# Dividing softmax weights ahead of their transposes in a hybrid attention layer

## The chip, the cores and the metric

The kernel runs on one core of a Trainium2 chip. The metric is the time of one execution on the device in microseconds, the median of three runs of the kernel. A profile is a further execution, recorded instruction by instruction. TensorE (PE) does matmuls and transposes, VectorE (DVE), ScalarE (ACT) and GpSimd (POOL) the elementwise work, and SyncE (SP) issues transfers. Each engine works through a queue of its own in a fixed order and waits on semaphores.

## The reference

One step of an encoder layer for 512 prompt rows and 64 sample rows (with 128 cached rows), 1024 wide: a projection, two kinds of attention with 8 heads of 64 each, an output projection, two layer norms, a feed-forward part of 4096 and a gated embedding.

```
def fox_attend(q, k, v, cum_q, cum_k, q_pos, k_pos):
    s = jnp.einsum('bqhd,blhd->bhql', q, k, ...) * HEAD_DIM ** -0.5
    decay = ...                       # sums of log forget gates, query less key
    p = jax.nn.softmax(jnp.where(mask, s + decay, NEG), axis=-1)
    return jnp.einsum('bhql,blhd->bqhd', p.astype(v.dtype), v)

def dsa_attend(q, k, v, iq, ik, iw, q_pos, k_pos, topk):
    # an indexer scores the keys: sum over index heads of iw * relu(iq . ik)
    _, sel = lax.top_k(score, topk)   # attention over the chosen keys alone
    ...
    x = layer_norm(ALPHA * x + jnp.einsum('blm,md->bld', mix, w_o), ln1_g, ln1_b)
    hid = jnp.square(jax.nn.relu(jnp.einsum('bld,df->blf', x, w_up)))
    x = layer_norm(ALPHA * x + jnp.einsum('blf,fd->bld', hid, w_down), ln2_g, ln2_b)
```

## The kernel before, in words

Prompt and sample are 576 columns, in two halves of 288. A float32 factor is split into a high part (rounded) and a low part (the rest), and each product is three matmuls (L274): high by high, high by low, low by high. Weights go through one queue of units: a load by SP (L155), a cast on ScalarE for the high part (L176), a subtraction on VectorE or, for some units, GpSimd for the low part (L180). The tiles are wraw and whl. Calls of WT.step(n) emit up to n such pieces between matmuls.

The heads are taken in eight pairs (p). Pairs 0 to 3 are forgetting attention, pairs 4 to 7 indexed attention. While pair p + 1 is projected (k, q, v, each 48 matmuls into one PSUM tile m), pair p is attended to by `ticks`: 9 jobs for each pair, prompt block i (128 queries, so 128 to 512 keys) of head hh, and one for the sample. A job passes through stages, one tick after another, in the order that PLAN writes out: qk (the scores, PSUM tile S), addmax (scores plus bias, and their maximum, on VectorE, L858), exp (ScalarE, L866, with the sum of the row), norm, ptrans (transposes of the weights sP into PSUM tile T), pevac (PT from T; ScalarE in pairs 0 to 3, VectorE in 4 to 7). After a pair's last job pv multiplies by the values into PSUM tiles V (prompt) and X (sample), and oevac writes the output's high and low parts, BH and BL. S, T and X share three PSUM banks.

Where the division lies: the sample's job divides its weights in norm (reciprocal L871, multiplication L872) ahead of its transposes. For the prompt the weights stay as they are. At a pair's last job, VectorE takes the reciprocals of all sums, ScalarE spreads them to 64 columns each (rows, L877), TensorE transposes them (four transposes, X<-ident,rows), ScalarE copies them out (R, L888), and oevac multiplies V by R (mix, L951); then ScalarE rounds mix to BH (L953) and GpSimd subtracts for BL (L954).

The evacuations of a projection (proj_evac) go into a list of delayed calls, of which three are made after each step of 6 matmuls. For q of pairs 1 to 3 these are: qs, the high part (ScalarE, L720), the low part (VectorE, L721), two pairs of transfers on SP's queue (L722, L723), the sample's queries QS out of the same m (ScalarE, L726), two casts on GpSimd (L727, L728).

Beside the first pairs runs the indexer (`choice`): its logits (L631 on TensorE, L634 a relu on ScalarE out of S or X, L637 and L639 a sum on VectorE), for the sample last (tiles cosT, sinT, dbiasS), and then top-k on VectorE (max, match_replace).

Behind pair 7: wo1 (six eighths of the output projection), wo2 for the halves A and B (the last two eighths; its evacuation, L1248, adds to Y and feeds the layer norm's sums), ple, the first feed-forward group, and so on. wo2 calls WT.step(4) after each of its 8 steps in half A and WT.step(0) in half B. A scheduler moves instructions within each engine's queue by its own estimate of times, so that the order below is not only that of the code.

Of the kernel before, what the change touches and what calls it, by code (L numbers as in the profile page):

```python
# [11 lines left out]
OP = mybir.AluOpType  # L12
# [24 lines left out]
def tile_hybrid_step(ctx: ExitStack, tc: tile.TileContext, I, O):  # L37
# [6 lines left out]
    def f(ap):  # L44
        return ap.bitcast(F32)
# [637 lines left out]
    def proj_evac(p, kind, m):  # L683
        g, pp = divmod(p, 4)
        v = m[:, :, :HW]
        P = pair[p]
        dly = [0]

        def q(fn, d=None):
            if d is not None:  # L690
                dly[0] = d
            later(dly[0], fn)

        def v2(ap):
# [12 lines left out]
        if g == 0:
            if kind == "q":
                P["q32s"] = QS[p % 2]
                P["Q2"] = Q2[p % 2]  # L710
                if p == 0:
                    q(lambda: ACT.mul(v2(QE[lo]), v[lo], sc))
                    q(lambda: ACT.mul(v2(QO[hi]), v[hi], sc))
                    q(lambda: DVE.scalar_tensor_tensor(v2(QE[hi]), v[lo], sc, f(v2(QE[lo])), op0=OP.mult, op1=OP.subtract))
                    q(lambda: DVE.scalar_tensor_tensor(v2(QO[lo]), v[hi], sc, f(v2(QO[hi])), op0=OP.mult, op1=OP.subtract))
                    src = (QE, QO)
                else:

                    qh, ql = [sb.tile([128, NT], F32R, name="qs", tag=t) for t in ("t2", "t1")]
                    q(lambda: ACT.mul(v2(qh), v, sc))  # L720
                    q(lambda: DVE.scalar_tensor_tensor(v2(ql), v, sc, f(v2(qh)), op0=OP.mult, op1=OP.subtract))  # L721
                    q(lambda: (SP.dma_start(f(QE[lo]), f(qh[lo])), SP.dma_start(f(QO[hi]), f(qh[hi]))))  # L722
                    q(lambda: (SP.dma_start(f(QE[hi]), f(ql[lo])), SP.dma_start(f(QO[lo]), f(ql[hi]))))  # L723
                    src = (qh, qh)
                for r in (lo, hi):
                    q(lambda r=r: ACT.mul(P["q32s"][r, r], m[r, 1, HW - NS:HW], sc))  # L726
                q(lambda: POOL.tensor_copy(P["Q2"][lo, 0], f(src[0][lo, :NP])))  # L727
                q(lambda: POOL.tensor_copy(P["Q2"][hi, 1], f(src[1][hi, :NP])))  # L728
                return
            k32 = sb.tile([128, NT], F32, name="k32", bufs=1)  # L730
            q(lambda: ACT.copy(v2(k32), v))
        else:
            state["k"] -= 4.0 if kind == "q" else 2.4
            x32 = sb.tile([128, NT], F32, name="x32", tag="k32" if kind == "k" else "t1")
            xr = sb.tile([128, NT], F32, name="xr", tag="t2")
            for r in range(4):
                s = r ^ 1
                q(lambda r=r, s=s: ACT.mul(v2(xr[r * 32:r * 32 + 32]), v[s * 32:s * 32 + 32], sc))
            q(lambda: DVE.scalar_tensor_tensor(v2(x32), v, sc, v2(cosT), op0=OP.mult, op1=OP.mult))
            q(lambda: DVE.tensor_tensor(xr, xr, sinT, OP.mult), 3)  # L740
            q(lambda: DVE.tensor_tensor(x32, x32, xr, OP.add), 3)
            if kind == "q":
                P["q32s"] = QS[p % 2]
                q(lambda: ACT.copy(QE[lo], x32[lo]), 5)
                q(lambda: ACT.copy(QO[hi], x32[hi]))
                q(lambda: DVE.tensor_tensor(QE[hi], x32[lo], f(QE[lo]), OP.subtract), 5)
                q(lambda: DVE.tensor_tensor(QO[lo], x32[hi], f(QO[hi]), OP.subtract))
                for r in (lo, hi):
                    q(lambda r=r: ACT.copy(P["q32s"][r, r], x32[r, NP:]))
                return  # L750
            k32 = x32
        P["k32"] = k32
        P["KL"] = KL = KLP[p % 2]
        P["k32s"] = sb.tile([128, NS], F32, name="k32s", bufs=2)
        q(lambda: ACT.copy(QE[lo], k32[lo]), 6 if g else 3)
        q(lambda: ACT.copy(QO[hi], k32[hi]))
        q(lambda: (SP.dma_start(f(QE[hi]), f(QE[lo])), SP.dma_start(f(QO[lo]), f(QO[hi]))))
        q(lambda: SP.dma_start(O["kT"][g, pp], k32))
        eng = POOL if p > 1 else DVE
        q(lambda: eng.tensor_tensor(KL[lo, 0], k32[lo, :NP], f(QE[lo, :NP]), OP.subtract))  # L760
        q(lambda: eng.tensor_tensor(KL[hi, 1], k32[hi, :NP], f(QO[hi, :NP]), OP.subtract))
        q(lambda: ACT.copy(P["k32s"], k32[:, NP:]))
# [97 lines left out]

    def exp(j):
        P = pair[j["p"]]
        if "sums" not in P:
            P["sums"] = sb.tile([128, 2, 4], F32, name="sums", bufs=2)
        s = j["st"][:, 2:3] if j["s"] else P["sums"][:, j["hh"], j["i"]:j["i"] + 1]
        ACT.activation(j["P"], j["P"], AF.Exp, bias=j["st"][:, 0:1], scale=-1.0, accum_out=s)  # L866

    def norm(j):

        if j["s"]:  # L870
            DVE.reciprocal(j["st"][:, 3:4], j["st"][:, 2:3])  # L871
            ACT.mul(j["P"], j["P"], j["st"][:, 3:4])  # L872
        elif j["last"]:
            sums = pair[j["p"]]["sums"]
            DVE.reciprocal(sums, sums)
# [2 lines left out]

    def scales(j):

        if not j["last"]:
            return
        rows = pair[j["p"]]["rows"]
        ps = psum_1("X", 1)
# [59 lines left out]
    def oevac(j):  # L944
# [485 lines left out]
    L1A = LayerNorm(A, 0, (4, 5, 2, 12))  # L1430
    L1B = LayerNorm(B, 0, (3, 8, 7, 12))
    L1 = both(L1A, L1B)
    drive(wo2(A, L1A, 4), 8, None, 0)
    early = fb.tile([128, 4], F32, name="ln_r", bufs=2)
    ACT.activation(early[:, 0:1], epst, AF.Sqrt, bias=epst[:, 0:1])
    drive(seq(wo2(B, L1B, 0), ple()), 24, L1, 24, False)
    drive(up(0, (L1A, L1B)), 16, L1, 16, False)
    XS = sums_of_x()
    n_xs = 11
# [152 lines left out]
```

## Time and profile before

| | |
|---|---|
| runs of the kernel | 787.88 us median, 787.68 to 787.93 |
| profiled execution | 789.02 us, of which the span of instructions is 787.2 us |
| mean granted TensorE clock | 0.998 |
| busy: TensorE, VectorE, ScalarE, GpSimd | 775.8, 543.9, 432.8, 98.4 us |
| pairs 1 to 3, 4 to 6, 7 | some 28 us each from 98 us on; 7 beside wo1, to 306 us |

A profile row reads: start and length in us (in a timeline), engine, line, operation, tiles written <- read, shape. In brackets stands how long the engine was idle before it and whose end it waited for. In a list of waits the figures are the total, how often, and the longest. "PEld" is the load of stationary weights, "SPq" the issue of a transfer. A group's two figures behind the bar are busy time in us and the mean of one in ns.

### The profile page before, as it was taken

To read this page: it belongs to the slowest core of one execution; us is meant where nothing else is said; L and a number is where in the kernel's file an instruction comes from. 1 tells how busy PE (TensorE), PEld (TensorE's weight loads), DVE (VectorE), ACT (ScalarE), POOL (GpSimd) and SP (SyncE) were. 2 spreads that over 40 slices of the span, in tenths; PEclk is the share of its full clock that TensorE was granted. 3 is DMA by queue.
4 is the path that set the end of the run, shared out by engine and by line. 5 is a ranking of instruction groups with operands and counts; after the bars stand their busy time and mean duration, and the time that the engine had idled before them with its cause. 6 is when DMAs were issued, how large, how long until landed. Compare 5 with 4: busy or idle time off the path is not lost.

```text
span 787.2 us, 14870 instructions
## 1 busy us (share of the span) xinstructions
PE 775.8 (99%) x5861; PEld 755.4 (96%) x5861; DVE 543.9 (69%) x1115; ACT 432.8 (55%) x911; POOL 98.4 (12%) x108
## 2 busy tenths in 40 slices
PE   8998999999999999999999999999999999999997
PEld 7987999999999998999999999999999999999997
DVE  6789978785457555999747749476594865647653
ACT  6477666788778444686425436253462634616351
POOL 4002345354332000100000000000000000010000
PEclk9999999999999999999999999999999999999999
DMA  7537343255213224332213223142221422730001
GB/s 268 174 54 156 92 118 103 80 155 196 91 58 102 76 81 157 138 122 87 101 54 111 91 70 106 55 134 81 78 85 55 134 81 81 250 109 31 27 28 67
DMA packets 30214, 81.44 MB, mean 103 GB/s; under 512 B 5056, under 2 KB 8896, under 8 KB 30016
## 3 DMA queue, kind: packets, MB, share of 16 engines
q1 hardware_dynamic: 30144, 80.49, 32.9%
q8 instruction: 46, 0.75, 0.4%
q14 instruction: 24, 0.20, 0.1%
HBM read 66.38 MB, written 9.54 MB: 96 GB/s over the span
## 4 chain that ended last, share of the span: by engine, by line
PE 87%; issue 5%; DVE 5%; ACT 1%; DMA 1%; POOL 0%; SPq 0%; DVEq 0%; ACTq 0%; POOLq 0%
PE g L274 57%; PE m L274 17%; PE n L274 2%; PE T L56 2%; PE V L941 2%; DVE dbias L639 1%; PE S L850 1%; PE S L848 1%; PE X L56 1%; DMA xraw<-in_xT_dram 1%; DVE whl L180 1%; PE m L432 1%; PE m L439 1%; PE S L439 1%; POOL BL L954 0%
## 5 line engine op out<-in xcount | busy, mean ns | idle before, releaser
L176 ACT CAST whl<-wraw 128x512 fp32r<-128x512 f32 (+1 forms) x214 | 127.6, 610 | 138.2 <-PE g L274 115.6
L274 PE MATMUL g<-BH,whl 128*128 128x288 f32 (+2 forms) x864 | 181.0, 297 | 0.8 <-DVE Y L1248 0.7
L274 PE MATMUL m<-AH,whl 128*128 128x288 f32 x736 | 177.4, 309 | 0.0
L180 DVE TENSOR_TENSOR whl<-wraw,whl 128x512 fp32r<-128x512 f32 (+1 forms) x180 | 121.0, 693 | 52.8 <-ACT whl L176 52.0
L274 PEld LDWEIGHTS g<-BH,whl 128*128 128x128 f32 x864 | 141.0, 188 | 2.8 <-DVE Y L1248 1.2
L274 PEld LDWEIGHTS m<-AH,whl 128*128 128x128 f32 x736 | 127.0, 190 | 1.9 <-issue 1.0
L274 PE MATMUL g<-BL,whl 128*128 128x288 f32 (+2 forms) x432 | 127.5, 296 | 0.0
L274 PE MATMUL m<-AL,whl 128*128 128x288 f32 x368 | 109.2, 297 | 0.0
L274 PE MATMUL g<-hidE,whl 128*128 128x288 f32 (+2 forms) x768 | 103.4, 295 | 0.0
L274 PE MATMUL g<-hidO,whl 128*128 128x288 f32 (+2 forms) x768 | 103.3, 295 | 0.0
L274 PEld LDWEIGHTS g<-hidO,whl 128*128 128x128 f32 x768 | 102.3, 188 | 0.0
L274 PEld LDWEIGHTS g<-hidE,whl 128*128 128x128 f32 x768 | 102.2, 188 | 0.1
L274 PEld LDWEIGHTS g<-BL,whl 128*128 128x128 f32 x432 | 81.3, 188 | 0.2
L274 PEld LDWEIGHTS m<-AL,whl 128*128 128x128 f32 x368 | 70.0, 190 | 0.7
L274 PE MATMUL g<-s,whl 128*128 128x288 f32 x432 | 68.5, 298 | 0.0
L274 PEld LDWEIGHTS g<-s,whl 128*128 128x128 f32 x432 | 60.1, 188 | 2.2 <-DVE u L1360 1.1
L176 ACT CAST whl<-wsum 128x512 fp32r<-128x512 f32 x36 | 22.2, 616 | 60.7 <-PE g L274 60.5
L1137 POOL TENSOR_TENSOR ln_s<-Y 128x576 f32<-128x576 f32 (+2 forms) x3 | 4.4, 1468 | 403.6 <-DVE Y L1422 391.2
L866 ACT ACTIVATE sP<-sP,st 128x128 f32<-128x128 f32 (+4 forms) x72 | 39.5, 550 | 25.7 <-DVE st L858 25.4
L1397 DVE SCALAR_TENSOR_TENSOR Y<-Y,g 128x576 f32<-128x576 f32 x48 | 36.0, 750 | 24.5 <-PE g L274 24.1
L180 POOL TENSOR_TENSOR whl<-wraw,whl 128x512 fp32r<-128x512 f32 x34 | 43.8, 1288 | 71.4 <-ACT whl L176 69.6
L180 DVE TENSOR_TENSOR whl<-wsum,whl 128x512 fp32r<-128x512 f32 x36 | 24.6, 687 | 27.4 <-ACT whl L176 27.4
(294 smaller groups left out, 1268.5 us busy)
## 6 DMA issues: line engine op xcount, KB each, us to landing
wraw<-in_w_up_dram SPq DMA_DIRECT2D x32, 512.0 KB, 3.5
wraw<-in_w_down_dram SPq DMA_DIRECT2D x32, 512.0 KB, 3.5
wraw<-in_w_qkv_dram SPq DMA_DIRECT2D x23, 512.0 KB, 4.2
wraw<-in_w_gate_dram SPq DMA_DIRECT2D x8, 512.0 KB, 4.5
wraw<-in_w_o_dram SPq DMA_DIRECT2D x8, 384.0 KB, 3.0
out_vT_dram<-v SPq DMA_DIRECT2D x8, 288.0 KB, 2.2
Y<-in_xT_dram SPq DMA_DIRECT2D x8, 288.0 KB, 6.1
PLD<-PL SPq DMA_DIRECT2D x4, 576.0 KB, 3.3
```

The costliest lines, as they stand in the source:

```text
L56: PE.transpose(out, in_, ident[:n, :n])
L176: ACT.copy(self.hv[h][0], src)
L180: eng.tensor_tensor(lv, src, f(hv), OP.subtract)
L274: PE.matmul(ps, W(w, kw, wc), a[:, ka, cols], start=(first and i == 0), stop=(last and i == n - 1))
L432: PE.matmul(mk[:, h, :HW], w0(part, k), a[:, k, h * HW:(h + 1) * HW], start=(k == 0 and i == 0), stop=(k == 7 and i == 2))
L439: PE.matmul(acc[b][:n[b], :304], a[:, k, b * 128:b * 128 + n[b]], ixw(part, k), start=(k == 0 and i == 0), stop=(k == 7 and i == 2))
L639: DVE.scalar_tensor_tensor(dst[:n, :nk], r[:n, :nk], w, dst[:n, :nk], op0=OP.mult, op1=OP.add)
L848: PE.matmul(ps[:, :n], Q[:, c], K[:, :n], start=True, stop=False)
L850: PE.matmul(ps[:, :n], Q[:, c], P["KL"][:, hh, :n], start=False, stop=True)
L866: ACT.activation(j["P"], j["P"], AF.Exp, bias=j["st"][:, 0:1], scale=-1.0, accum_out=s)
L941: PE.matmul(ps[r, x * 256 + c.start:x * 256 + c.stop], P["vt"][:, kb, r], t[:, hh, kb, c], start=(kb == 0), stop=(kb == n - 1))
L1397: later(0, lambda y=y, m=m, s=s: DVE.scalar_tensor_tensor(y, y, s, m[:, :, :HW], op0=OP.mult, op1=OP.add))
```

## The change

Pairs 1 to 7 now divide as the sample's job does: norm takes each job's reciprocal (VectorE) and multiplies the weights by it, on ScalarE in pairs 1 to 3 and on VectorE (tensor_scalar) in pairs 4 to 7, ahead of the transposes. For them rows, its transposes, R and mix are gone: oevac rounds V and X straight to BH (ScalarE) and subtracts for BL (VectorE, no longer GpSimd). Pair 0 keeps the old way. Three more edits: the sample's queries QS are read out of m ahead of the low part; the low parts of weight unit 7 (pair 2's q) are made on VectorE and no longer on GpSimd; wo2 takes 3 pieces in half A and 1 in half B for each step.

```
-            U[kind, p] = WT.add(qkv[p * 3 + x], pool_l=(p * 3 + x > 6))
+            U[kind, p] = WT.add(qkv[p * 3 + x], pool_l=(p * 3 + x > 7))
...
+                def qs():
+                    for r in (lo, hi):
+                        q(lambda r=r: ACT.mul(P["q32s"][r, r], m[r, 1, HW - NS:HW], sc))
                 if p == 0:
                     q(lambda: ACT.mul(v2(QE[lo]), v[lo], sc))
                     q(lambda: ACT.mul(v2(QO[hi]), v[hi], sc))
+                    qs()
...
                     q(lambda: ACT.mul(v2(qh), v, sc))
+                    qs()
                     q(lambda: DVE.scalar_tensor_tensor(v2(ql), v, sc, f(v2(qh)), op0=OP.mult, op1=OP.subtract))
...
-                for r in (lo, hi):
-                    q(lambda r=r: ACT.mul(P["q32s"][r, r], m[r, 1, HW - NS:HW], sc))
...
-        s = j["st"][:, 2:3] if j["s"] else P["sums"][:, j["hh"], j["i"]:j["i"] + 1]
+        s = j["st"][:, 2:3] if j["s"] or j["p"] else P["sums"][:, j["hh"], j["i"]:j["i"] + 1]
...
-        if j["s"]:
-            DVE.reciprocal(j["st"][:, 3:4], j["st"][:, 2:3])
-            ACT.mul(j["P"], j["P"], j["st"][:, 3:4])
+        if j["s"] or j["p"]:
+            r = j["st"][:, 3:4]
+            DVE.reciprocal(r, j["st"][:, 2:3])
+            if j["s"] or j["p"] < 4:
+                ACT.mul(j["P"], j["P"], r)
+            else:
+                DVE.tensor_scalar(j["P"], j["P"], r, None, op0=OP.mult)
         elif j["last"]:
...
-        if not j["last"]:
+        if j["p"] or not j["last"]:
             return
...
+        if p:
+            for c, v in ((slice(0, NP), ps), (slice(NP, NT), pss[:, :NS])):
+                ACT.copy(BH[:, p, c], v)
+                DVE.tensor_tensor(BL[:, p, c], v, f(BH[:, p, c]), OP.subtract)
+            return
...
-    drive(wo2(A, L1A, 4), 8, None, 0)
+    drive(wo2(A, L1A, 3), 8, None, 0)
-    drive(seq(wo2(B, L1B, 0), ple()), 24, L1, 24, False)
+    drive(seq(wo2(B, L1B, 1), ple()), 24, L1, 24, False)
```

The change moves instructions at three places that matter below. The lines of the new kernel are a few higher. The first is ScalarE's queue where the indexer's last logits meet pair 1's q (qs, QS_161) and pair 0's jobs; before:

```order
L634 ACTIVATE work<-X 128x512 [waits DVE_49,PE_49]
L919 COPY PT<-T 128x2x128 [waits PE_49]
L720 ACTIVATE qs<-m 128x576 [waits PE_49]
L634 ACTIVATE cosT<-S 64x192 [waits PE_49]
L176 CAST whl<-wraw 128x512
L726 ACTIVATE QS_161<-m 64x64 [waits DVE_49]
L726 ACTIVATE QS_161<-m 64x64
L634 ACTIVATE cosT<-X 64x192 [waits PE_49]
L634 ACTIVATE sinT<-S 64x192 [waits PE_49]
L866 ACTIVATE sP,sums<-sP,st 128x384 [waits DVE_49]
L919 COPY PT<-T 128x2x128 [waits PE_49]
```

The same place now:

```order
L870 ACTIVATE sP,sums<-sP,st 128x384 [waits DVE_49]
L725 ACTIVATE qs<-m 128x576 [waits PE_49]
L634 ACTIVATE cosT<-S 64x192 [waits PE_49]
L714 ACTIVATE QS_161<-m 64x64
L176 CAST whl<-wraw 128x512
L714 ACTIVATE QS_161<-m 64x64
L634 ACTIVATE cosT<-X 64x192 [waits PE_49]
L870 ACTIVATE sP,sums<-sP,st 128x384 [waits DVE_49]
L634 ACTIVATE sinT<-S 64x192 [waits PE_49]
L927 COPY PT<-T 128x2x128 [waits PE_49]
```

QS waits for VectorE no more, and pair 0's exp, which does wait for it, has come ahead of sinT<-S.

The second is VectorE's queue at the same time; before:

```order
L639 SCALAR_TENSOR_TENSOR dbias_110<-work,iw,dbias_110 128x512 [waits DVE_49,Activation_49]
L658 MEMSET dbias_109 64x64
L639 SCALAR_TENSOR_TENSOR dbias_110<-work,iw,dbias_110 128x512 [waits DVE_49,Activation_49] x4
L721 SCALAR_TENSOR_TENSOR qs<-m,qs 128x576 [waits DMAHW2_49,Activation_49]
L637 TENSOR_SCALAR dbiasS<-cosT,iw 64x192 [waits Activation_49]
L858 ISA sP,st<-S,causal 128x384 [waits PE_49]
```

The same place now (L862 is addmax):

```order
L639 SCALAR_TENSOR_TENSOR dbias_110<-work,iw,dbias_110 128x512 [waits DVE_49,Activation_49]
L180 TENSOR_TENSOR whl<-wraw,whl 128x512 [waits DMAHW1_49,Activation_49]
L639 SCALAR_TENSOR_TENSOR dbias_110<-work,iw,dbias_110 128x512 [waits DVE_49,Activation_49] x3
L637 TENSOR_SCALAR dbiasS<-cosT,iw 64x192 [waits Activation_49]
L862 ISA sP,st<-S,causal 128x384 [waits PE_49]
L862 ISA st 128x1
L727 SCALAR_TENSOR_TENSOR qs<-m,qs 128x576 [waits DMAHW2_49,Activation_49]
L180 TENSOR_TENSOR whl<-wraw,whl 128x512
```

The low part L721 (now L727) went behind addmax, and a low half of unit 7 came in ahead. On TensorE the fourth of the sample's logits (X<-fox) waits for VectorE now and for ScalarE before, and has one matmul of L274 ahead of it in place of three.

The third is VectorE's queue at the end of wo1 and the start of wo2; before:

```order
L951 TENSOR_TENSOR mix_4032<-V,R 128x512
L180 TENSOR_TENSOR whl<-wraw,whl 128x512
L1087 SCALAR_TENSOR_TENSOR Y<-Y,m 128x576
L180 TENSOR_TENSOR whl<-wraw,whl 128x512 x5
L1248 TENSOR_TENSOR Y<-g,Y 128x2x288
L180 TENSOR_TENSOR whl<-wraw,whl 128x512 x2
L1248 TENSOR_TENSOR Y<-g,Y 128x2x288 x2
```

The same place now (L1261 is wo2's evacuation):

```order
L961 TENSOR_TENSOR BL<-X,BH 128x64
L961 TENSOR_TENSOR BL<-V,BH 128x512
L180 TENSOR_TENSOR whl<-wraw,whl 128x512 x4
L1100 SCALAR_TENSOR_TENSOR Y<-Y,m 128x576
L180 TENSOR_TENSOR whl<-wraw,whl 128x512
L1261 TENSOR_TENSOR Y<-g,Y 128x2x288
L180 TENSOR_TENSOR whl<-wraw,whl 128x512 x2
L1261 TENSOR_TENSOR Y<-g,Y 128x2x288
```

Five low halves stand ahead of the first L1261 where six stood ahead of L1248, four of them ahead of wo1's last evacuation, and BL is made here.

More of the change, by code (lines that the diff above doesn't have):

```diff
@@ L862, in exp @@
         P = pair[j["p"]]
-        if "sums" not in P:
+        if j["p"] == 0 and "sums" not in P:
             P["sums"] = sb.tile([128, 2, 4], F32, name="sums", bufs=2)
-        s = j["st"][:, 2:3] if j["s"] else P["sums"][:, j["hh"], j["i"]:j["i"] + 1]
+        s = j["st"][:, 2:3] if j["s"] or j["p"] else P["sums"][:, j["hh"], j["i"]:j["i"] + 1]
         ACT.activation(j["P"], j["P"], AF.Exp, bias=j["st"][:, 0:1], scale=-1.0, accum_out=s)
     def norm(j):
-        if j["s"]:
-            DVE.reciprocal(j["st"][:, 3:4], j["st"][:, 2:3])
-            ACT.mul(j["P"], j["P"], j["st"][:, 3:4])
+        if j["s"] or j["p"]:
[5 more added lines that the diff above has]
+                DVE.tensor_scalar(j["P"], j["P"], r, None, op0=OP.mult)
         elif j["last"]:
```

## The prediction

> **What bounds the kernel now.** I read the page's busy line first, then a table of stretches, then TensorE's waits, and then the timeline round each wait.
>
> ```profile
> span 787.2 us, 14870 instructions
> ...
> PE 775.8 (99%) x5861; PEld 755.4 (96%) x5861; DVE 543.9 (69%) x1115; ACT 432.8 (55%) x911; POOL 98.4 (12%) x108
> ```
>
> TensorE works in 775.8 of 787.2 us, so time can come from two places alone: work taken off TensorE, and the 11.4 us in which it stands, most of which lies at the start and the end. The table of stretches has start and end, length, then busy time of PE, PEld, DVE, ACT and POOL, and the granted clock.
>
> ```profile
> 98.00:126.00 28.00, 28.00 (x229) 26.99 (x227) 22.90 (x73) 18.48 (x48) 12.58 (x11) 1.00 0.36 108
> 126.00:154.00 28.00, 28.00 (x228) 26.92 (x226) 21.47 (x65) 19.56 (x52) 11.91 (x12) 1.00 0.35 99
> 154.00:182.00 28.00, 28.00 (x229) 26.98 (x227) 19.76 (x50) 24.42 (x59) 12.87 (x11) 1.00 0.55 171
> 182.00:210.00 28.00, 28.00 (x229) 27.00 (x227) 14.47 (x36) 21.14 (x50) 11.71 (x9) 1.00 0.34 110
> 270.00:310.00 40.00, 40.00 (x318) 38.53 (x315) 19.89 (x41) 16.01 (x35) 2.88 (x2) 1.00 0.27 88
> 310.00:342.00 32.00, 31.23 (x232) 30.46 (x231) 31.30 (x57) 23.18 (x46) 3.33 (x2) 1.00 0.44 156
> ```
>
> Where pairs 1 to 7 are attended to (98 to 310), TensorE never stops, and no other engine is full; ScalarE comes nearest in pair 3 (24.42 of 28). Behind it, at 310 to 342, VectorE is full (31.30 of 32). TensorE's waits from 60 us on are three:
>
> ```profile
> PE X L631 <- ACT cosT L634: 2.1, 1, 2.1
> PE g L274 <- DVE Y L1248: 0.7, 1, 0.7
> PE X L631 <- ACT PT L919: 0.7, 1, 0.7
> ```
>
> The two at L631 (the sample's index logits) lie in the first of these two stretches, and behind them the clock falls:
>
> ```profile
> 72.00:76.90 4.90, 2.09 (x15) 1.42 (x13) 4.33 (x9) 2.46 (x10) 2.89 (x3) 1.00 0.88 228
> 76.90:80.50 3.60, 3.60 (x17) 3.58 (x17) 2.10 (x8) 1.77 (x7) 0.00 (x0) 0.53 0.51 171
> ```
>
> A mean clock of 0.53 over 3.6 us loses 1.7 us. So this place costs 2.8 us of idle time and 1.7 us of slow clock, 4.5 us in all. Who causes it stands on ScalarE's and VectorE's timelines:
>
> ```profile
> 73.91 0.45 ACT L726 ACTIVATE QS<-m 64x64 f32<-64x64 f32 x2 [1.67 <-DVE qs L721]
> 74.38 0.32 ACT L634 ACTIVATE cosT<-X 64x192 f32<-64x192 f32 x1
> ```
>
> ```profile
> 72.30 0.91 DVE L639 SCALAR_TENSOR_TENSOR dbias<-work,iw,dbias 128x512 f32<-128x512 f32 x1
> 73.14 0.74 DVE L721 SCALAR_TENSOR_TENSOR qs<-m,qs 128x576 fp32r<-128x576 f32 x1
> 73.80 1.34 DVE L637 TENSOR_SCALAR dbiasS<-cosT,iw 64x192 f32<-64x192 f32 x1
> 75.07 0.54 DVE L858 CUSTOM_DVE_ANT_0 sP<-S,causal 128x384 f32<-128x384 f32 x1
> ```
>
> Pair 1's read of sample's queries (L726) waits for the low part (L721), VectorE is late with that, and behind L726 on ScalarE's queue stands the logits' evacuation (L634) for which TensorE waits.
>
> **The change, part by part.** *The transposes of the sums.* In pairs 1 to 7 four transposes each go. One group, on TensorE's timeline:
>
> ```profile
> 297.44 0.29 PE L274 MATMUL m<-BL,whl 128*128 128x288 f32 x1
> 297.57 0.29 PE L274 MATMUL m<-BH,whl 128*128 128x288 f32 x1
> 297.70 0.60 PE L56 MATMUL X<-ident,rows 128*128 128x128 f32 x4
> 298.06 0.38 PE L274 MATMUL m<-BH,whl 128*128 128x288 f32 x1
> 298.28 0.30 PE L274 MATMUL m<-BL,whl 128*128 128x288 f32 x1
> ```
>
> Matmuls start every 0.13 us. From 297.57 to 298.28 there would be two such steps, 0.27, and there are 0.71: the group costs 0.44. Seven make 3.1 us, all of it gained, since the stretches above have no idle time to hide it. At the least (0.36, if the 0.09 at the return to matmuls stays with another group) it is 2.5. I take 3.1.
>
> *The sample's queries.* L726 moves ahead of the low part (p 0 to 3). The 1.67 us wait goes, but this is not all that TensorE waits for. In the new order TensorE's X<-fox waits for VectorE: it takes the bank of pair 0's last 384-wide scores, which addmax (0.54) frees. VectorE reached L721 at 73.14. In the new order L637 stands there, and one low half of unit 7 (0.60) has come ahead of it. Against that, unit 7's halves no longer run on GpSimd:
>
> ```profile
> 70.37 1.28 POOL L180 TENSOR_TENSOR whl<-wraw,whl 128x512 fp32r<-128x512 f32 x1 [0.56 <-POOL biasS L598]
> ```
>
> ```profile
> 73.77 1.26 POOL L180 TENSOR_TENSOR whl<-wraw,whl 128x512 fp32r<-128x512 f32 x1
> ```
>
> ```profile
> L639 DVE SCALAR_TENSOR_TENSOR dbias<-work,iw,dbias x12: 609/746/1705, 59.7 to 72.3; 128x512 f32<-128x512 f32 x7, 128x384 f32<-128x384 f32 x5
> ```
>
> ```profile
> L637 DVE TENSOR_SCALAR dbias<-work,iw x3: 353/411/480, 52.2 to 64.0; 128x256 f32<-128x256 f32 x1, 128x384 f32<-128x384 f32 x1, 128x512 f32<-128x512 f32 x1
> ```
>
> The one L639 of 1.71 us (median 0.75) runs beside the first, and L637, 0.48 for 512 columns, takes 1.34 for 192 beside the second. If GpSimd is the reason, 0.96 us goes: L637 starts at 73.14 + 0.60 - 0.96 = 72.8, ends after 0.4, addmax 0.54 later, and TensorE starts at 73.7 and not at 74.76. If not, it starts at 74.7. Two matmuls (0.27) now stand behind this wait and no longer ahead. So the first wait shrinks by -0.2 to 0.8; I take 0.6, nearer to the end where GpSimd is the reason, since two slowed instructions speak for it. The second wait (0.7) was for a PT copy behind the same jam; pair 0's exp now stands ahead of sinT<-S on ScalarE and waits for the same addmax, so I leave 0.1 of it and take 0.6, from 0 to 0.7. The low part and SP's qE and qO transfers behind it come one step later; pair 1's scores read them only after the 48 matmuls (6.2 us) of v: 0. Idle time: 1.2 us gained (-0.2 to 1.5). With 1.6 us of idle time in place of 2.8, the clock probably does not fall (1.7 us, or 0). Together 2.9.
>
> The Trainium skill's page "TensorE: Matmul & The Clock Gate" (section "What's actually happening") says that the clock halves after at least one idle window of about 3.4 us. By that rule neither the old nor the new wait would lower the clock, and the sum stays as it is here; the trace has it lowered behind waits of 2.1 and 0.7 us with work between, so the measurement decides and the fall may come again.
>
> *Steps of wo2.* A takes 3 weight pieces for each step and not 4, B 1 and not 0: eight pieces move from A to B. VectorE and ScalarE now:
>
> ```profile
> 308.28 3.09 DVE L180 TENSOR_TENSOR whl<-wraw,whl 128x512 fp32r<-128x512 f32 x5
> 311.30 0.74 DVE L1248 TENSOR_TENSOR Y<-g,Y 128x576 f32<-128x576 f32 x1
> ```
>
> ```profile
> 306.36 1.14 ACT L176 CAST whl<-wraw 128x512 fp32r<-128x512 f32 x2 [1.55 <-POOL BL L954]
> ```
>
> Five low halves (0.6 each) stand ahead of the first L1248, for which TensorE waits 0.73, which with the way back into step is 0.9. The new order has one low half less ahead of it. And the casts waited 1.55 us for GpSimd's BL of the last pair, which is gone, as is SP's wait for it ahead of a w_up load. L1248 comes 0.6 to 2.1 us earlier: the wait goes. I take 0.9 (0, if a wait for weights takes its place in B, to 1.3, if VectorE's later lateness shrinks too). Beyond 342 nothing is touched.
>
> *Division ahead of the transposes, pairs 1 to 3 (ScalarE).* Each pair gets eight multiplications and eight reciprocals, and loses two copies; BH from V costs what BH from mix did. Prices:
>
> ```profile
> L866 ACT ACTIVATE sP<-sP,st 128x128 f32<-128x128 f32 (+4 forms) x72 | 39.5, 550 | 25.7 <-DVE st L858 25.4
> ```
>
> ```profile
> L877 ACT COPY rows<-sums x8: 617/618/625, 88.2 to 290.2; 128x512 f32<-128x512 f32 x8
> ```
>
> ```profile
> L888 ACT COPY R<-X x8: 585/587/590, 95.3 to 298.3; 128x512 f32<-128x512 f32 x8
> ```
>
> ```profile
> L871 DVE RECIPROCAL st<-st x8: 152/158/164, 79.1 to 282.4; 128x1 f32<-128x1 f32 x8
> ...
>   ACT sP L872: 2.3, 6
> ```
>
> At the exps' mean of 0.55 the eight cost 4.4, less 0.62 and 0.59: 3.2 us of ScalarE more in each pair. Each also waits for its reciprocal; the sample's job, which already divides so, waited 2.3 us in six cases, 0.39 each: eight make 3.1. Pair 3 then has 24.42 + 3.2 + 3.1 = 30.7 us of ScalarE in 27.6. The 3.1 us too many meet this slack, at pair 3's tightest job:
>
> ```profile
> 165.79 0.19 ACT L866 ACTIVATION_READ_ACCUMULATOR sP<-sP,st 128x1 f32 x1
> ```
>
> ```profile
> 168.66 0.27 PE L56 MATMUL T<-ident,sP 128*128 128x128 f32 x1
> ```
>
> From the end of the exp (165.98) to its transpose there are 2.7 us. So I charge 0.4 (0 to 2.0); in pairs 1 and 2 ScalarE stays under 26 of 27.6. Queued behind a waiting multiplication are PT copies and weight casts.
>
> *Pairs 4 to 7 (VectorE)*: eight reciprocals (0.16) and eight tensor_scalars (0.41, the median of L637's) make some 4.6 us on 14.47 of 28: hidden, 0. What else goes (mix on VectorE, BL on GpSimd) or moves (QS in pairs 2, 3) costs nothing, since TensorE waits for none of it there.
>
> *Sum*: -3.1 - 1.2 - 1.7 - 0.9 + 0.4 = -6.5 us. The profiled execution took 789.02 us for its span of 787.2; the median of the runs is 787.88, and I subtract from that: **781.4 us**.
>
> **Rivals.** *The clock still falls* (chance 0.30): 1.6 us of idle time is enough when they lie in one stretch. Sum without the 1.7: **783.1**. For it speaks that 2.8 with work between was enough; against it, that the 0.7 us before 312 was not.
>
> *ScalarE's handoffs set pairs 1 to 3* (slower, 0.05): on VectorE's queue the reciprocal stands between top-k instructions, and if that makes each wait 0.9 us and not 0.39, ScalarE needs 18.48 + 3.2 + 7.2 = 28.9, 30.0 and 34.8 us for 27.6: 10.9 too many, less 2.7 of slack, 8.2 stalls TensorE, and 787.88 - 6.9 + 8.2 = **789.2**. It is slower from 0.9 us for each handoff on; the 0.39 measured speaks against it.
>
> *GpSimd holds up the new tensor_scalars in pairs 4 and 5* (0.07): like L637's. GpSimd is busy 42% of that stretch (11.71 of 28), so of sixteen some seven meet it, and lose 0.64 on average, 4.3 us. If TensorE paid it all: 781.4 + 4.3 = **785.7**. Against it: VectorE is half idle there. The Trainium skill's "GPSIMD Engine Reference" (section "1. Specifications") says that GpSimd shares its SBUF interfaces with VectorE and meets instructions in a 2-port mode or with two SBUF inputs; L637's 1.34 us agrees with it.
>
> *The jams only move* (0.08): L631 waits as long for addmax as for ScalarE, weights are late in B, ScalarE costs 1.5: -3.1 + 1.5 gives **786.3**, and with the bound of 2.5 no change that can be told.
>
> **How the numbers follow.** The forecast has 0.50. Its own range, 780.0 to 782.5, takes the bounds of the wo2 and logits waits. About 0.2% (1.6 us) is what a measurement of this kernel can tell from no change. Forecast, falling clock and held-up tensor_scalars are all faster, and half of the moved jams: 0.90; the other half and a mild handoff jam are the same: 0.05; slower 0.05. The range reaches from 779.4 (all idle time at 72 to 77 gone) to 784.7 (falling clock with 1.6 us of ScalarE's stall).
>
> **What would show it.** Right: no L726 wait for L721, TensorE's wait at L631 under 1.7 us in sum, a clock of 1.00 from 72 to 82, no wait for Y at 305 to 312, pairs 1 to 7 at 27.5 to 27.8 us each with no idle TensorE. Wrong: a new TensorE wait for sP or PT between 95 and 300, above all in pair 3; a clock of 0.5 behind 77; or a wait for whl in wo2's B.

## The result, and the profile after

The changed kernel takes **781.61 us** (median of 6 runs, 780.43 to 783.4), the kernel before 787.9 (6 runs, 786.93 to 788.86): a ratio of 0.992, 95% interval 0.9905 to 0.9935, which leaves out 1. The forecast was 781.4.

The page of the changed kernel, its first lines:

```profile
span 780.5 us, 14883 instructions
...
PE 771.8 (99%) x5833; PEld 752.5 (96%) x5833; DVE 561.2 (72%) x1205; ACT 435.2 (56%) x921; POOL 85.8 (11%) x99
```

TensorE is busy 4.0 us less (part of that is the slow clock, under which the same matmuls stay busy longer) and the span is 6.7 shorter, so some 2.7 us of idle time went as well. The table of stretches of the changed kernel (start and end, length, busy time of PE, PEld, DVE, ACT, POOL, the granted clock, share and rate of the transfers):

```profile
72.00:76.90 4.90, 3.28 (x25) 2.85 (x24) 4.76 (x13) 3.02 (x11) 1.24 (x2) 1.00 0.67 204
76.90:80.50 3.60, 3.60 (x29) 3.51 (x27) 3.40 (x12) 1.72 (x6) 0.00 (x0) 1.00 0.84 250
98.00:126.00 28.00, 28.00 (x227) 26.92 (x226) 24.60 (x85) 21.76 (x58) 12.89 (x11) 1.00 0.37 109
154.00:182.00 28.00, 28.00 (x225) 26.70 (x225) 20.29 (x61) 25.47 (x62) 11.50 (x11) 1.00 0.57 191
182.00:210.00 28.00, 28.00 (x227) 26.93 (x227) 19.39 (x55) 20.76 (x48) 10.86 (x9) 1.00 0.30 94
310.00:342.00 32.00, 31.81 (x238) 31.21 (x237) 31.10 (x61) 25.66 (x53) 3.14 (x2) 1.00 0.37 140
```

The slow stretch behind 77 us is gone from this execution (1.00 where 0.53 stood). ScalarE's extra work in pair 1 is as priced (21.76 for 18.48), and in the stretch of pair 3, the fullest, it is busy for 25.47 of 28; VectorE's extra work is as priced too (19.39 for 14.47 in 182 to 210, 4.9 more). TensorE's waits from 60 us on are two:

```profile
PE X L631 <- DVE st L862: 1.6, 1, 1.6
...
PE g L274 <- DVE Y L1261: 0.2, 1, 0.2
```

Where the 6.7 us came from can be read off four instructions that stand at the same place of both programs: the first transposes of L496, the first projection matmul behind pair 0's last V, the one behind pair 7's, and the first matmul of w_down. On TensorE's timeline before:

```profile
34.58 0.50 PE L496 MATMUL T<-identr,kstack 128*128 128x128 f32 x2 [0.29 <-DVE kstack L492]
99.28 0.40 PE L274 MATMUL m<-AH,whl 128*128 128x288 f32 x1
303.16 0.40 PE L274 MATMUL m<-BH,whl 128*128 128x288 f32 x1
387.21 0.69 PE L274 MATMUL g<-hidE,whl 128*128 128x288 f32 x4
```

And after:

```profile
34.97 0.51 PE L496 MATMUL T<-identr,kstack 128*128 128x128 f32 x2 [0.28 <-DVE kstack L492]
96.18 0.40 PE L274 MATMUL m<-AH,whl 128*128 128x288 f32 x1
297.19 0.40 PE L274 MATMUL m<-BH,whl 128*128 128x288 f32 x1
380.51 0.69 PE L274 MATMUL g<-hidE,whl 128*128 128x288 f32 x4
```

Up to the first row the changed kernel is 0.4 later (the loads at the start scatter by more than that from run to run). The stretch with pair 0 and the indexer shrinks from 64.70 to 61.21 (-3.49), pairs 1 to 7 from 203.88 to 201.01 (-2.87), wo2 to w_down from 84.05 to 83.32 (-0.73). Behind that both need 399.99 to the end of the span.

### The profile page after: what moved, and what is told of

Same layout as the page of the kernel before. It is cut to its first block, busy times and chain, and to the rows that moved or that the text cites. A ratio compares the mean times of both kernels' runs of the same rounds, so it can differ in the third digit from the quotient of the medians.

```text
span 780.5 us, 14883 instructions
## 1 busy us (share of the span) xinstructions
PE 771.8 (99%) x5833; PEld 752.5 (96%) x5833; DVE 561.2 (72%) x1205; ACT 435.2 (56%) x921; POOL 85.8 (11%) x99
## 4 chain that ended last, share of the span: by engine, by line
PE 93%; DVE 4%; ACT 1%; issue 1%; DMA 0%; SPq 0%; DVEq 0%; ACTq 0%
PE g L274 56%; PE m L274 21%; PE T L56 3%; PE n L274 2%; PE V L949 2%; PE S L854 1%; PE S L852 1%; DVE dbias L639 1%; PE m L432 1%; PE S L439 1%; PE m L439 1%; PE X L56 1%; ACT work L634 0%; PE X L439 0%; DMA iraw<-in_w_idx_dram 0%
## 5 line engine op out<-in xcount | busy, mean ns | idle before, releaser
L274 PE MATMUL g<-BH,whl 128*128 128x288 f32 (+2 forms) x864 | 180.7, 297 | 0.0
L274 PE MATMUL m<-AH,whl 128*128 128x288 f32 x736 | 176.4, 307 | 0.0
L274 PEld LDWEIGHTS g<-BH,whl 128*128 128x128 f32 x864 | 141.0, 188 | 1.6 <-ACT u L1371 1.1
L274 PEld LDWEIGHTS m<-AH,whl 128*128 128x128 f32 x736 | 126.3, 188 | 1.9 <-issue 1.0
L274 PE MATMUL g<-BL,whl 128*128 128x288 f32 (+2 forms) x432 | 127.5, 296 | 0.0
L274 PE MATMUL m<-AL,whl 128*128 128x288 f32 x368 | 109.0, 296 | 0.0
L274 PE MATMUL g<-hidE,whl 128*128 128x288 f32 (+2 forms) x768 | 103.4, 295 | 0.0
L274 PE MATMUL g<-hidO,whl 128*128 128x288 f32 (+2 forms) x768 | 103.4, 296 | 0.0
L274 PEld LDWEIGHTS g<-hidO,whl 128*128 128x128 f32 x768 | 102.4, 188 | 0.0
L274 PEld LDWEIGHTS g<-hidE,whl 128*128 128x128 f32 x768 | 102.2, 188 | 0.1
L274 PEld LDWEIGHTS g<-BL,whl 128*128 128x128 f32 x432 | 81.3, 188 | 0.2
L274 PEld LDWEIGHTS m<-AL,whl 128*128 128x128 f32 x368 | 69.6, 189 | 0.7
L274 PE MATMUL g<-s,whl 128*128 128x288 f32 x432 | 68.4, 299 | 0.0
L274 PEld LDWEIGHTS g<-s,whl 128*128 128x128 f32 x432 | 60.1, 188 | 2.2 <-DVE u L1373 1.2
L176 ACT CAST whl<-wsum 128x512 fp32r<-128x512 f32 x36 | 22.2, 616 | 60.7 <-PE g L274 60.5
L180 POOL TENSOR_TENSOR whl<-wraw,whl 128x512 fp32r<-128x512 f32 x32 | 41.3, 1292 | 76.9 <-ACT whl L176 58.6
```

The lines of the kernel that those rows point to most:

```text
L176: ACT.copy(self.hv[h][0], src)
L180: eng.tensor_tensor(lv, src, f(hv), OP.subtract)
L274: PE.matmul(ps, W(w, kw, wc), a[:, ka, cols], start=(first and i == 0), stop=(last and i == n - 1))
```

## The experiments

Each time is the median of 6 to 12 executions; the two kernels under "The clock" ran once each and are not in the table. The table has the ratio to executions of the kernel before taken beside them (medians 787.2 to 787.9) with its 95% interval, and from one profiled execution of each the stretch with pair 0 ("front", from the first row above to the second), the sum of pairs 1 to 7, wo2 to w_down, TensorE's waits at L631 (and the transposes beside it), and whether the clock fell to 0.50 behind them:

| kernel | time | ratio | front | pairs 1-7 | wo2 | waits | clock fell |
|---|---|---|---|---|---|---|---|
| before | 787.9 | 1 | 64.70 | 203.88 | 84.05 | 2.12 + 0.70 | yes |
| changed | 781.61 | 0.9905-0.9935 | 61.21 | 201.01 | 83.32 | 1.62 | no |
| division alone | 783.53 | 0.9941-0.9973 | 63.70 | 201.11 | 83.31 | 1.85 + 0.09 | yes |
| queries alone | 786.09 | 0.9972-0.9993 | 63.03 | 203.88 | 84.05 | 1.54 + 0.37 | yes |
| unit 7 alone | 784.28 | 0.9951-0.9977 | 60.75 | 203.88 | 84.06 | 1.00 | no |
| steps alone | 786.85 | 0.9984-1.0008 | 63.20 | 203.88 | 83.83 | 1.84 | yes |
| changed, queries late | 780.85 | 0.9896-0.9935 | 61.07 | 201.11 | 83.32 | 1.03 | no |
| changed, pairs 1-3 on VectorE | 783.24 | 0.9923-0.9964 | 62.08 | 202.59 | 83.33 | 1.62 | no |
| changed, GpSimd two inputs | 782.93 | 0.9922-0.9962 | 61.87 | 201.03 | 83.33 | 2.37 | no |
| changed, GpSimd one input | 781.3 | 0.990-0.994 | 62.46 | 201.05 | 83.31 | 1.70 | yes |
| queries late, pair 0 divides | 781.28 | 0.9905-0.9942 | 61.51 | 201.13 | 83.33 | 1.10 | no |

Before, the division alone and the steps alone have the same instructions on TensorE in the front, in the same order, and on the other engines but for the first multiplications of pair 1 at its end: 64.70, 63.70 and 63.20 are three executions of it, 63.87 on average. By that mean the change gained 2.7 us there, and by the first profile alone 3.5.

**The parts, each alone.** First the division (exp, norm, scales and oevac as in the change, the rest as before):

```
-        if j["s"]:
+        if j["s"] or j["p"]:
...
-        if not j["last"]:
+        if j["p"] or not j["last"]:
             return
...
+        if p:
+            for c, v in ((slice(0, NP), ps), (slice(NP, NT), pss[:, :NS])):
...
```

> The kernel before with the division alone (pairs 1 to 7 divide ahead of the transposes, no transposed rows, BH and BL straight from PSUM); queries, unit 7 and wo2's steps as before. My terms: seven groups of transposes, -3.1, plus 0.4 of ScalarE's stall in pair 3; the waits of 2.1 and 0.7 at L631 and the fallen clock (0.53 in 77 to 80.5) stay; and the 1.55 that wo2's casts waited for GpSimd's BL goes, which by itself should take most of TensorE's 0.9 at Y. Predicted -2.7 without and -3.6 with that: 784.3 to 785.2. Rival (the steps, not BL, made the wait for Y): the wait of 0.7 for Y stays and the time is 785.2. Rival (the division also mends the jam at 72): under 783.

Measured 783.53, some 3.4 us less than before by the ratio. The pairs give 2.77, and wo2 gives 0.74 with its steps untouched:

```profile
PE X L631 <- ACT cosT L634: 1.9, 1, 1.9
...
PE g L274 <- DVE Y L1257: 0.2, 1, 0.2
```

The wait for Y of 0.7 has become 0.2: VectorE makes BL itself and the casts no longer stand behind GpSimd. On ScalarE's timeline eight of them run with no idle time ahead, where the casts waited 1.55 before:

```profile
298.85 4.28 ACT L176 CAST whl<-wraw 128x512 fp32r<-128x512 f32 x8
```

The jam at 72 stays.

Next the queries, the `qs()` of the change alone:

```
                     q(lambda: ACT.mul(v2(qh), v, sc))
+                    qs()
                     q(lambda: DVE.scalar_tensor_tensor(v2(ql), ...))
...
-                for r in (lo, hi):
-                    q(lambda r=r: ACT.mul(P["q32s"][r, r], ...))
```

> The kernel before with sample's queries read ahead of the low part, alone; unit 7's low halves stay on GpSimd. My theory (the wait of QS for the low part was the cause): the wait of L714 for L727 is gone, TensorE's waits at L631 shrink from 2.8 to 1.6 or 2.0, and the clock stays at 1.00 in 72 to 82: 785.0 to 785.4. Rival (the halves on GpSimd were the cause): waits still 2.3 to 2.8, and L639 and L637 still have single durations of 1.7 and 1.3; the clock falls or not with them: 787.4 to 787.9.

Measured 786.09. QS waits for nothing any more, but TensorE stops for 1.54 and 0.37 us all the same, for addmax and for the relu of the logits, and the clock falls. Its waits and VectorE's timeline:

```profile
PE X L631 <- DVE st L862: 1.5, 1, 1.5
...
PE T L56 <- ACT cosT L634: 0.4, 1, 0.4
```

```profile
66.87 4.47 DVE L639 SCALAR_TENSOR_TENSOR dbias<-work,iw,dbias 128x512 f32<-128x512 f32 x4
```

Four sums of the logits take 4.47, some 1.7 more than the 0.67 each by which undisturbed ones follow one another. Each of the two theories was half right: the wait of QS went, and the time moved little (some 1.3 us by the ratio).

Then unit 7 alone:

```
-            U[kind, p] = WT.add(qkv[p * 3 + x], pool_l=(p * 3 + x > 6))
+            U[kind, p] = WT.add(qkv[p * 3 + x], pool_l=(p * 3 + x > 7))
```

> The kernel before with unit 7's low halves on VectorE, alone; QS still waits for the low part. If GpSimd's TENSOR_TENSORs slowed L639 (1.71) and L637 (1.34), these go back to about 0.75 and 0.4, VectorE reaches the low part some 1 us earlier in spite of one more half (0.60), and the waits at L631 fall from 2.8 to 1.6 or 2.0 without any move of the queries: 785.0 to 785.4 with the clock at 1.00, 786.7 if it falls. Rival (the two were slow for another reason): the two halves add 1.2 on VectorE, the waits grow to 3.4 or more: 788.5.

Measured 784.28, with QS still behind the low part. That is more than was expected (785.0 to 785.4), and the front of 60.75 is shorter even than the 61.21 of the changed kernel. ScalarE's and VectorE's timelines of this kernel:

```profile
72.04 0.45 ACT L726 ACTIVATE QS<-m 64x64 f32<-64x64 f32 x2 [0.30 <-DVE qs L721]
```

```profile
69.99 0.69 DVE L180 TENSOR_TENSOR whl<-wraw,whl 128x512 fp32r<-128x512 f32 x1
70.60 0.75 DVE L639 SCALAR_TENSOR_TENSOR dbias<-work,iw,dbias 128x512 f32<-128x512 f32 x1
71.26 0.75 DVE L721 SCALAR_TENSOR_TENSOR qs<-m,qs 128x576 fp32r<-128x576 f32 x1
71.93 1.10 DVE L639 SCALAR_TENSOR_TENSOR dbias<-work,iw,dbias 128x512 f32<-128x512 f32 x1
72.95 0.30 DVE L637 TENSOR_SCALAR dbiasS<-cosT,iw 64x192 f32<-64x192 f32 x1
73.18 0.54 DVE L858 CUSTOM_DVE_ANT_0 sP<-S,causal 128x384 f32<-128x384 f32 x1
```

QS waits 0.30 and not 1.67, since VectorE comes to the low part at 71.26 and not at 73.14, though it has a low half more to make. L637 takes 0.30 where it took 1.34.

Last the steps of wo2 (A 3, B 1):

```
-    drive(wo2(A, L1A, 4), 8, None, 0)
+    drive(wo2(A, L1A, 3), 8, None, 0)
...
```

> The kernel before with wo2's steps alone (A 3, B 1). My term: -0.9, from 0 to -1.3: 787.0. The casts still wait 1.55 for GpSimd's BL; if that wait rather than the five low halves ahead of the first sum Y makes TensorE stand, this kernel gains nothing and the kernel with the division alone gains the 0.9: 787.9.

Measured 786.85, not told apart from before by the time; the profile gives 0.22 (84.05 to 83.83; TensorE's wait for Y is 0.4 and the casts still wait 1.56 for GpSimd's BL), and beside the division they add nothing (83.31 without, 83.32 with).

**The queries taken back** out of the changed kernel (the diff of the queries above, reversed):

> The changed kernel with sample's queries read behind the low part again; division, unit 7 on VectorE and wo2's steps stay. The theory after the first four runs: unit 7's two halves leaving GpSimd mended the jam at 72, and the move of the queries adds nothing. From the first wait for L496's transposes (about 34 us) to the last V of pair 0 there were 61.0 us in the changed kernel and 60.55 in the kernel with unit 7's move alone: then this one has 60.5, TensorE waits 1.0 at L631 and the clock stays: 0.4 to 0.5 less than the changed kernel, 781.2. Rival, the prediction's reason (L726's wait for the low part makes TensorE stand): waits of 2 or more at L631 come back and the clock falls, 783.5.

Measured 780.85, its interval on that of the changed kernel. The stop is 1.03, the clock stays behind it, and the front is 61.07 for 61.21 (60.5 was expected). The rival falls: without the halves on GpSimd the old place of the queries does no harm, and the new place does no measurable good.

**Is it GpSimd?** One more instruction on GpSimd in the changed kernel, released by the same qs as its casts:

```
+    if p == 1:
+        scr = sb.tile([128, NT], F32, name="mix32", tag="mix32")
+        q(lambda: POOL.tensor_tensor(scr[:, :512], f(qh[:, :512]), causal, OP.add))
     q(lambda: POOL.tensor_copy(P["Q2"][lo, 0], f(src[0][lo, :NP])))
```

> The changed kernel with one more TENSOR_TENSOR on GpSimd (128x512, two inputs in SBUF, its result is not used), ahead of its two casts of pair 1's queries, so that it runs from 71.6 to 72.9 beside VectorE's L639 and L637; TensorE's order is the same and VectorE's is up to addmax. If it slows VectorE as unit 7's halves seemed to, L639 or L637 take 0.5 to 1.0 longer, TensorE's wait of 1.62 at L631 grows to 2.1 to 2.6, and the clock falls to 0.5 for 3.4 us: 781.6 + 0.5 to 1.0 + 1.7, that is 783.8 to 784.3. Rival (VectorE was slow for another reason): wait and time as they are, 781.6.

In the other kernel two copies stand there (`POOL.tensor_copy(scr[:, :512], f(qh[:, ...]))`):

> The same with two copies of 128x512 on GpSimd (one input each, results not used) in place of the TENSOR_TENSOR. If only instructions with two inputs collide, VectorE keeps its durations (L637 about 0.4 to 0.66) and the wait stays 1.6 and the time 781.6. If any work on GpSimd collides, the wait grows by 0.3 to 1.0, and the clock falls from about 1.7 us of wait on: 782 to 784.3.

VectorE's three L639 ahead of L637, in the changed kernel, then with the two-input instruction (and that instruction on GpSimd), then with the copies:

```profile
70.13 2.70 DVE L639 SCALAR_TENSOR_TENSOR dbias<-work,iw,dbias 128x512 f32<-128x512 f32 x3
72.75 0.66 DVE L637 TENSOR_SCALAR dbiasS<-cosT,iw 64x192 f32<-64x192 f32 x1
73.34 0.53 DVE L862 CUSTOM_DVE_ANT_0 sP<-S,causal 128x384 f32<-128x384 f32 x1
```

```profile
69.41 3.45 DVE L639 SCALAR_TENSOR_TENSOR dbias<-work,iw,dbias 128x512 f32<-128x512 f32 x3
71.05 1.27 POOL L733 TENSOR_TENSOR mix<-qs,causal 128x512 f32<-128x512 f32 x1 [2.69 <-ACT qs L725]
```

```profile
69.63 2.78 DVE L639 SCALAR_TENSOR_TENSOR dbias<-work,iw,dbias 128x512 f32<-128x512 f32 x3
```

The added TENSOR_TENSOR cost VectorE 0.75 us, and TensorE's stop grew by just that, from 1.62 to 2.37. The copies cost 0.08. But they don't show one-input work to be harmless: GpSimd's casts come later by the first copy, so that L639 has GpSimd beside it for some 1.1 us in both kernels (71.67 to 72.8 in the changed one, 71.26 to 72.4 here), and L637 took 0.66 beside a cast in the changed kernel and 0.30 beside nothing.

In the two profiles the clock did the opposite of what was expected: it stayed behind 2.37 and fell behind 1.70. So the kernel with the longer stop has the shorter front in its profile. One profile is one execution, though. The mean granted clock of every execution is on record, and a window of 3.41 us at 0.50 takes 0.002 off it, so that an execution at 0.999 or above had none while TensorE worked (0.998 can be one behind the last matmul). That holds for one of six executions with the TENSOR_TENSOR, the profiled one, and for three of six with the copies. It holds for five of six of the changed kernel, for all eight with unit 7 alone, and for 13 of 49 of the kernel before. By the median the two-input kernel is 1.3 us slower than the changed one, where 2.2 to 2.7 were expected.

**The clock.** To get more stops, chains of multiplications by 1 were put ahead of sums of w_down in the changed kernel (work on top of the kernel's own):

```
+            n = {1: [9, 10, 9, 11, 10, 12, 0, 0], 5: [0, 0, 10, 0, 11, 9, 0, 0]}.get(j, [0] * 8)[g]
+            if n:
+                later(0, lambda m=m, n=n: [DVE.tensor_scalar(m[:, :, :HW], m[:, :, :HW], 1.0, ...) for _ in range(n)])
```

> The changed kernel with nine chains of 9 to 12 multiplications by 1 on VectorE, in place in PSUM, ahead of sums of w_down in the FFN: each holds TensorE up for some time there, where it otherwise never stands. The question is the clock, since a stop of 2.37 us left it at 1.00 and one of 1.70 did not. If TensorE's idle time is counted in fixed windows of about 3.4 us and the clock is 0.5 for one window after a window with 1.6 to 1.7 us of idle time or more, then every stop over 3.4 us is followed by a slow stretch of 3.4 us, stops between 1.7 and 3.4 by some and not by others, those below 1.5 that stand alone by none, and slow stretches begin at multiples of about 3.4 us from one another. Rival (the length of one stop decides): all stops over one length, none below it. The time is beside the point: some 10 to 40 us over 781.6.

Only one chain made TensorE stop, for 2.14 us at 604, and the clock stayed (782.58 us in one run): a window's border cut the idle time into 1.00 and 1.14. With chains of 11 to 14:

> The changed kernel with twelve chains of 11 to 14 multiplications by 1 on VectorE in the FFN (nine of 9 to 12 made TensorE stop but once, for 2.14 us, and left the clock at 1.00). So far single stops of 2.37, 2.14 and 1.62 left the clock, and 1.85, 1.84 and 1.70 did not. If fixed windows of about 3.4 us decide, of stops between 1.7 and 3.4 some are followed by a slow stretch of about 3.4 us and others not, with no order by length, and every stop over 5 us is followed by one. Rival (the length of a stop, or what runs beside it, decides): an order by length shows. 790 to 820 us.

802.47 us in one run, with stops of 0.72, 1.38, 3.07, 3.64, 5.82 and 1.64. All changes of the granted clock within a profile lie at multiples of 3.41 us from one another (in the kernel before at 76.97 and 80.38). Cut into such windows, the idle time of a window (3.41 less PE busy, the first figure) can be set against the clock of the next. Before, with the copies, the changed kernel, with the TENSOR_TENSOR, and three places of the last kernel:

```profile
73.56:76.97 3.41, 1.51 (x9) 1.08 (x9) 2.90 (x8) 2.29 (x9) 1.39 (x2) 1.00 0.84 187
76.97:80.38 3.41, 3.41 (x15) 3.39 (x16) 1.95 (x7) 1.58 (x7) 0.00 (x0) 0.50 0.50 171
```

```profile
70.73:74.14 3.41, 1.71 (x13) 1.31 (x12) 3.31 (x7) 2.37 (x9) 2.82 (x4) 1.00 0.79 251
74.14:77.55 3.41, 3.41 (x18) 3.38 (x17) 3.28 (x10) 1.97 (x8) 0.50 (x1) 0.50 0.56 133
```

```profile
71.19:74.60 3.41, 1.79 (x14) 1.40 (x14) 3.31 (x7) 2.46 (x9) 1.57 (x2) 1.00 0.78 238
74.60:78.01 3.41, 3.41 (x28) 3.19 (x27) 3.14 (x11) 2.33 (x10) 0.00 (x0) 1.00 0.61 147
```

```profile
69.51:72.92 3.41, 2.09 (x15) 1.69 (x13) 3.20 (x4) 2.74 (x9) 1.88 (x2) 1.00 0.88 245
72.92:76.33 3.41, 2.36 (x17) 2.15 (x18) 3.28 (x9) 1.98 (x7) 1.02 (x2) 1.00 0.45 113
76.33:79.74 3.41, 3.41 (x28) 3.32 (x27) 3.27 (x14) 1.80 (x6) 0.00 (x0) 1.00 0.85 230
```

```profile
460.29:463.71 3.42, 2.12 (x16) 1.88 (x15) 3.42 (x7) 0.62 (x1) 0.00 (x0) 1.00 0.00 0
463.71:467.12 3.41, 1.64 (x12) 1.64 (x13) 2.31 (x4) 0.00 (x0) 0.00 (x0) 1.00 0.00 0
467.12:470.53 3.41, 3.38 (x24) 2.99 (x23) 1.69 (x4) 1.68 (x4) 0.00 (x0) 1.00 0.19 46
...
552.45:555.87 3.42, 0.56 (x4) 0.57 (x5) 3.42 (x7) 0.00 (x0) 0.00 (x0) 1.00 0.00 0
555.87:559.28 3.41, 3.41 (x16) 3.41 (x15) 3.41 (x7) 0.00 (x0) 0.00 (x0) 0.50 0.00 0
...
665.09:668.50 3.41, 1.76 (x14) 1.54 (x13) 3.41 (x6) 0.62 (x1) 0.00 (x0) 1.00 0.00 0
```

Idle times of 1.90 and 1.70 in one window were followed by a window at 0.50; 1.62, 1.65, and 1.32 and 1.05 (the 2.37 us stop, cut in two by the border) were not. The same cut gives 1.80 for the division alone, 1.84 for the steps alone and 1.70 for the queries alone, and the clock fell behind all three. Behind one of 1.77 it did not (463.71), nor behind one of 1.74 at the end of the changed kernel (774.33 to 777.75), so the bound lies near half a window and is no sharper than 0.1 us in these records. The length of one stop does not decide: 3.07 us passed, 1.70 did not.

**The multiplications elsewhere.** In pairs 1 to 3 on VectorE:

```
-            if j["s"] or j["p"] < 4:
+            if j["s"]:
                 ACT.mul(j["P"], j["P"], r)
```

> The changed kernel with the division of pairs 1 to 3 on VectorE too (tensor_scalar, as in pairs 4 to 7). If ScalarE's eight multiplications and handoffs cost pair 3 its 0.23 us (28.00 from V to V against 27.77 in the pairs beside it), pair 3 comes to 27.77 and the time to 781.4. Rival (VectorE's top-k instructions stand ahead of the tensor_scalars in pairs 1 to 3, each 0.4 or more): TensorE waits for sP there, and pairs 1 to 3 take 28 us or more: 782 to 783.

Measured 783.24, and the rival holds. TensorE's waits have two new rows:

```profile
PE X L940 <- DVE st L862: 1.3, 1, 1.3
PE S L852 <- DVE st L862: 0.7, 1, 0.7
```

Both are for addmax, which stands behind top-k and tensor_scalars on VectorE; with the first pair 1 takes 29.13 in place of 27.78, and the second lies near the end of the front. Ahead of each a tensor_scalar of 128 columns ran beside a TENSOR_TENSOR of GpSimd and took 0.85 and 1.25 us, where undisturbed ones take 0.27 to 0.29. The one ahead of the first on VectorE's and GpSimd's timelines:

```profile
119.78 0.85 DVE L880 TENSOR_SCALAR sP<-sP,st 128x128 f32<-128x128 f32 x1
119.26 1.29 POOL L180 TENSOR_TENSOR whl<-wraw,whl 128x512 fp32r<-128x512 f32 x1 [6.12 <-PE S L854]
```

So GpSimd probably had a part in both stops; no run tests how much.

Pair 3 stayed at 28.00, but not by the same instruction. In the changed kernel it loses its 0.23 us at one place, on TensorE's and ScalarE's timelines:

```profile
170.48 0.66 PE L56 MATMUL T<-ident,sP 128*128 128x128 f32 x4
169.40 0.71 ACT L878 ACTIVATE sP<-sP,st 128x512 f32<-128x512 f32 x1
170.16 0.26 ACT L918 COPY PTs<-T 64x128 f32<-64x128 f32 x1
```

The transposes start 0.29 behind the matmul ahead of them, where 0.13 is the rhythm, just after a copy out of T (done at 170.42) that stands behind a multiplication in ScalarE's queue. With the multiplications on VectorE they follow by 0.13, and a later group of transposes (176.97) loses the time instead. That ScalarE's multiplications cost the changed kernel these 0.23 us is read from the order in time; no recorded wait says it.

**Pair 0 too** divides (on ScalarE, the queries late; `if True` for the conditions on p):

> The kernel with the queries late again, and pair 0 divides ahead of its transposes too (ScalarE), so that no rows of sums are left at all. By the price of the other pairs the eighth group of transposes gives 0.44: from L496's first transpose to the last V of pair 0 there are 60.4 us in place of 60.9, and 780.4 in all. Rival (pair 0 is where VectorE and ScalarE are full: VectorE was busy 14.95 of 16 us from 82 to 98): eight reciprocals and eight multiplications more (0.15 and 0.55 each) come on top of the logits and the top-k, TensorE waits for sP or X there, and the stretch takes 62 us or more: 782 or more.

Measured 781.28, no gain over the kernel with the queries late; the front is 61.51 for 61.07 though TensorE has four transposes less in it. TensorE's timelines of the two kernels, laid side by side, show that the transposes gave what they were priced at: 14.14 us in place of 14.56 from behind the jam to past their place. The same matmuls and transposes in another order took 6.31 in place of 5.40 in the jam, though (71.02 to 76.42 with the queries late, 69.91 to 76.22 here), and the granted clock was 1.00. Why, the runs don't show. A new stop of 0.17 ahead of pair 0's X came on top. No version was told apart from the changed kernel as faster.

## Why the prediction was right

**The transposes** (-3.1, and 0.4 of ScalarE's stall): right. Pairs 1, 2, 4 and 5 took 28.20 to 28.22 and take 27.77 or 27.78, from the first projection matmul behind one pair's last V to the next; that is 0.43 to 0.44 for each group. Pairs 6 and 7 shrank by the same, but are longer than the "some 28 us" given above: 30.58 and 32.22 before, 30.14 and 31.78 now. Pair 3 lost 0.23 against the 0.4 charged. The handoffs cost less than worked out: 0.39 for each of 24 would have been 9.4, and all multiplications together waited

```profile
ACT sP L878 <- DVE st L876: 4.6, 10, 0.7
```

4.6 us, in 10 of 32. The rival of the handoffs had no ground.

**wo2** (-0.9): measured -0.73; a wait of 0.2 for Y stays. Of the two causes named, the casts' wait for GpSimd's BL was the one; the steps alone give 0.22, and nothing beside it.

**The jam at 72** (-1.2 idle, -1.7 clock): the sum was right, -2.7 by the mean of three executions of the old code, and the stop left over is 1.62 where 1.6 was forecast. The step that failed is what the gain is put down to: the part counts it to L726 moving ahead of the low part. With that move alone the wait of 1.67 went, as said, but TensorE still stopped for 1.54 and 0.37 and the clock still fell; unit 7 without it did the whole. The 1.67 was where VectorE's lateness came to light, and VectorE was late since GpSimd worked beside it. The prediction had this as an "if" inside the queries' step and took most of it; it belonged at the head, as a term of unit 7's own. The row of 1.34 for an L637 that takes 0.48 at more than twice the columns was the evidence. That the number came out all the same is in part luck: the change held both edits.

**The clock**: that it would stay was right in the profile and in at least five of six executions, and near the edge: 1.62 us of idle time in a window, where 1.70 was enough in two other kernels. The clause that stops with work between lowered it while 0.7 did not was the right kind of evidence; missing was that the borders of the windows have a part in it, so that the old stops didn't lower it in every execution either (13 of 49 without). The Trainium skill's page "TensorE: Matmul & The Clock Gate" (section "What's actually happening") says that the window is free-running, which the steps of 3.41 us agree with. By its rule that the clock halves after at least one idle window the old stop of 2.12 could not have lowered the clock, and these runs show that about half a window of idle time is enough.

**VectorE's and ScalarE's extra work** in pairs 4 to 7 cost TensorE nothing, as said: no engine is seen to wait for L880. The rival that GpSimd holds up the new tensor_scalars was right in part: of the sixteen in pairs 4 and 5, two took 1.38 beside a GpSimd instruction (0.34 to 0.35 at that width otherwise) and two 0.71 (for 0.49), 2.5 us in all where 4.3 was priced. But TensorE paid none of it: both pairs take 27.77, like pairs 1 and 2, whose multiplications are on ScalarE.

## What to carry to other kernels

Where TensorE never stops, a group of its instructions is worth just the slots it takes from the neighbours' rhythm, and that can be read off a few rows. Where it stops, look for the instruction that is slower than its like, not for the queue on which the wait is written, and try edits at one place one by one, since they stand in for each other. A TensorE stop of under 2 us can cost twice its length, by a slow window behind it, or not, by where the border of a window falls; so judge the clock by several executions and not by one profile.

## What the runs showed of the hardware that was not expected

- The granted clock is 0.50 or 1.00 and changes at multiples of 3.41 us. While the kernels still had work for TensorE, a window with 1.70 us or more of idle TensorE was followed by one at 0.50 in eight of nine cases (the ninth had 1.77), one with up to 1.65 never. A slow window costs 1.7 us when TensorE has work.
- VectorE beside GpSimd: L637 (one input in SBUF, 192 columns) took 0.30 alone, 0.66 beside a cast and 1.34 beside a TENSOR_TENSOR that had started 0.03 ahead of it, but 0.30 where it had started 0.15 ahead of one (queries alone); three L639 (two inputs in SBUF) took 3.45 for 2.70 with a TENSOR_TENSOR of 1.27 more beside them; addmax and the low part, which have one of two inputs in PSUM, took 0.53 to 0.55 and 0.68 to 0.75 in all these kernels. The Trainium skill's "GPSIMD Engine Reference" (section "1. Specifications") says that GpSimd shares its SBUF interfaces with VectorE and meets VectorE's instructions in a 2-port mode or with two SBUF inputs. L639 is of the second kind and agrees; whether L637 ran in a 2-port mode, no run here shows.
